# Head norms and memory softmax in place in PSUM, small copies and scalings on ScalarE: a two-layer decoder trunk

## Chip, core and metric

The kernel runs as one program on one core of a Trainium2 chip. The core has TensorE (PE, matmuls into PSUM), VectorE (DVE), ScalarE (ACT), GpSimd (POOL), SyncE (SP, which issues the DMAs), an SBUF and a PSUM of eight banks of 512 fp32 words a partition. The metric is the device time of one execution in microseconds; less is better.

## What is computed

Two decoder layers over 512 tokens of width 1024, and 256 memory tokens. Layer 0 has a gated MLP, a differential attention (8 heads, two score maps each) and a memory cross-attention; layer 1 a convolution branch, a sparse attention and a memory cross-attention. Cut to what the change touches:

```python
def rms_norm(x, g):
    y = xf * lax.rsqrt(jnp.mean(xf * xf, axis=-1, keepdims=True) + EPS)
    return (y * g).astype(x.dtype)

# differential attention: p = softmax(q k^T), two maps of a head
pd = p[:, :, 0] - lam * p[:, :, 1]
o  = einsum('bhqk,bhkd->bhqd', pd, v)

# memory attention, 4 heads of 64
q, k = rms_norm(q, qnorm), rms_norm(k, knorm)
p = jax.nn.softmax(einsum('bshd,bmhd->bhsm', q, k) * HEAD_DIM ** -0.5)
y = einsum('bhsm,bmhd->bshd', p, v)
```

Queries and keys of the differential and of the sparse attention get a partial rotary embedding behind their norm.

## The kernel before

Weights come as 512 KB units by DMA and are split into a high and a low fp32r half (L376 on ACT, L377 on POOL for weights, on DVE for activations read from PSUM). A product is three matmuls (`mm3`, L396 to L398). Projections with tokens on the partitions (`proj_N`) leave each 128-token tile in a PSUM bank of kind "d"; those with features on the partitions (`proj_T`) fill a whole bank.

`head_norm` takes such a PSUM tile `p`: ACT squares it to SBUF (L492), DVE sums (L494), POOL makes the factor `r` by two tiny operations (`rstd`, L370 and L372), and DVE multiplies by the gain or by the rotary table, reading PSUM and writing an SBUF tile `t` (L498, L501), with the rotary parts added in SBUF (L503 to L505). `to_keys` (L511) and `to_queries` (L521) multiply `t` by `r`, SBUF to SBUF, and PE transposes the result (L393). `b_qk` does the same for the differential attention (L873 to L883).

`b_attn` runs 8 heads; in each, the four 128-query tiles in the order 3, 2, 1, 0: scores on PE (L923), mask and row minimum on DVE (L925), exponentials on ACT (L954), reciprocal (L955), the factor `cf` from the two row sums and `nlam`, minus lambda (L957), the difference of the two maps (L958), transposes (L393), a copy (L934) and the output matmuls (L961) into one bank of kind "o" per head.

`m_attn` takes two heads at a time: scores into a bank of kind "s" (L597, L598), row maximum on DVE (L600), two exponentials on ACT from PSUM to an SBUF tile `e` (L603), reciprocal (L604), and two scalings of `e` by `times`: the first on DVE (L572), the second on POOL (L570). Then transposes, a split and the products with the values (L582 to L584). `gate_heads` (L578) multiplies the output by its gate.

`c_taps` is the depthwise convolution of layer 1: four feature tiles of 31 taps. Three of them run on DVE (L1252, then 30 times L1260, accumulating in one PSUM bank of kind "c"), the second on ACT and POOL (L1257, L1258). Each tile begins when its two products are there (L1238 reads the second); the next DVE tile waits for the "c" bank. The taps have a low priority.

The program is written as generators that `merge` interleaves: `b_attn` with the projections of layer 0; `m_attn` of layer 0 with an output projection; in layer 1 `m_attn` with the convolution's projections (`glu`), then `d_kv`, `d_cmp` and `d_q`, then the sparse attention `d_attn`. The order on each engine is not written out by hand: the framework places the instructions by priority on a timeline of its own while it builds, so other instructions or other dependencies can give another order. Engines run their own queues in order and wait on semaphores; the framework orders accesses of two engines to one PSUM bank, where one of them writes, by such waits.

## Time and profile before

| | us |
|---|---|
| three runs | 743.29, 743.4, 739.89; median 743.29 |
| the profiled execution | 742.06 |
| its span in the trace | 740.3 |
| PE busy | 679.5 (92%) |
| DVE busy | 530.4 (72%) |
| ACT busy | 366.7 (50%) |
| POOL busy | 390.5 (53%) |

The profile is of one execution. Its span runs from the first to the last instruction; 1.76 us of its time lie around the span. PE is in use nearly throughout, but unevenly: the table by stage among the rows below shows where it waits. Times in the rows are us from the start of the span unless they are marked as a mean in ns.

### The profile page before, as it was taken

To read this page: it belongs to the slowest core of one execution; us is meant where nothing else is said; L and a number is where in the kernel's file an instruction comes from. 1 tells how busy PE (TensorE), PEld (TensorE's weight loads), DVE (VectorE), ACT (ScalarE), POOL (GpSimd) and SP (SyncE) were. 2 spreads that over 40 slices of the span, in tenths; PEclk is the share of its full clock that TensorE was granted. 3 is DMA by queue.
4 is the path that set the end of the run, shared out by engine and by line. 5 is a ranking of instruction groups with operands and counts; after the bars stand their busy time and mean duration, and the time that the engine had idled before them with its cause. 6 is when DMAs were issued, how large, how long until landed. Compare 5 with 4: busy or idle time off the path is not lost.

```text
span 740.3 us, 10929 instructions
## 1 busy us (share of the span) xinstructions
PE 679.5 (92%) x3819; PEld 574.2 (78%) x3819; DVE 530.4 (72%) x1216; ACT 366.7 (50%) x819; POOL 390.5 (53%) x343
## 2 busy tenths in 40 slices
PE   5999999999999898999899898896679989999997
PEld 3889998788898777888787687674457878778876
DVE  5507798777777697853669939999436776889774
ACT  5345345565565564633444465523413646575541
POOL 3376985645347487425565599856143423421440
PEclk9999999999999999999999999999688999999999
DMA  8442244542231434212223112041021100120111
GB/s 315 151 150 78 60 149 119 173 137 91 72 115 58 170 123 163 86 58 62 86 96 105 57 32 84 1 145 55 0 85 58 58 29 30 58 84 3 58 71 72
DMA packets 22375, 66.55 MB, mean 90 GB/s; under 512 B 3504, under 2 KB 3760, under 8 KB 22320
## 3 DMA queue, kind: packets, MB, share of 16 engines
q1 hardware_dynamic: 22320, 65.86, 26.9%
q8 instruction: 30, 0.49, 0.3%
q14 instruction: 25, 0.20, 0.1%
HBM read 57.46 MB, written 2.10 MB: 80 GB/s over the span
## 4 chain that ended last, share of the span: by engine, by line
PE 61%; DVE 25%; POOL 5%; ACT 4%; issue 3%; DMA 1%; SPq 0%; ACTq 0%; DVEq 0%; POOLq 0%
PE banks L397 16%; PE banks L396 15%; PE banks L398 15%; PE banks L393 5%; DVE banks L1260 4%; DVE arena_r L377 3%; PE banks L923 3%; ACT arena_r L376 2%; PE banks L1211 2%; POOL arena_r L377 2%; POOL arena_f L372 2%; DMA arena_f<-in_wall_dram 1%; DVE arena_f L925 1%; DVE arena_f L572 1%; POOL arena_f L1258 1%
## 5 line engine op out<-in xcount | busy, mean ns | idle before, releaser
L396 PE MATMUL banks<-arena_r 128*128 128x512 f32 (+2 forms) x784 | 293.7, 381 | 14.4 <-DVE arena_f L473 4.8
L397 PE MATMUL banks<-arena_r 128*128 128x512 f32 (+2 forms) x784 | 293.8, 377 | 4.9 <-POOL arena_r L377 4.8
L377 POOL TENSOR_TENSOR arena_r<-arena_f,arena_r 128x1024 fp32r<-128x1024 f32 (+2 forms) x87 | 211.7, 2442 | 161.5 <-ACT arena_r L376 160.9
L398 PE MATMUL banks<-arena_r 128*128 128x512 f32 (+2 forms) x784 | 292.3, 376 | 1.1 <-POOL arena_r L377 1.1
L396 PEld LDWEIGHTS banks<-arena_r 128*128 128x128 f32 x784 | 151.3, 194 | 40.2 <-DVE arena_f L473 6.2
L397 PEld LDWEIGHTS banks<-arena_r 128*128 128x128 f32 x784 | 151.9, 194 | 30.1 <-POOL arena_r L377 6.4
L398 PEld LDWEIGHTS banks<-arena_r 128*128 128x128 f32 x784 | 151.6, 194 | 25.4 <-POOL arena_r L377 2.0
L376 ACT ACTIVATE arena_r<-arena_f 128x1024 fp32r<-128x1024 f32 (+2 forms) x131 | 110.3, 854 | 94.4 <-PE banks L398 27.7
L393 PE MATMUL banks<-const,arena_f 128*128 128x128 f32 x507 | 84.8, 284 | 29.4 <-DVE arena_f L521 9.4
L393 PEld LDWEIGHTS banks<-const,arena_f 128*128 128x128 f32 x507 | 62.7, 147 | 41.1 <-DVE arena_f L521 9.9
L376 ACT ACTIVATE arena_r<-banks 128x512 fp32r<-128x512 f32 (+1 forms) x112 | 58.2, 532 | 55.9 <-PE banks L393 41.6
L377 DVE TENSOR_TENSOR arena_r<-banks,arena_r 128x512 fp32r<-128x512 f32 (+1 forms) x112 | 67.1, 606 | 21.0 <-ACT arena_r L376 20.6
L925 DVE CUSTOM_DVE_ANT_0 arena_f<-banks,const 128x512 f32<-128x512 f32 (+3 forms) x128 | 60.5, 483 | 29.1 <-PE banks L923 17.0
L570 POOL TENSOR_SCALAR arena_f<-arena_f 128x256 f32<-128x256 f32 (+3 forms) x48 | 29.8, 627 | 90.9 <-DVE arena_f L1190 49.2
L372 POOL TENSOR_TENSOR arena_f<-arena_f,const 128x4 f32<-128x4 f32 (+3 forms) x60 | 68.5, 1143 | 3.7
L1260 DVE SCALAR_TENSOR_TENSOR banks<-arena_f,const,banks 128x482 f32<-128x482 f32 (+14 forms) x90 | 66.0, 733 | 1.6
L954 ACT ACTIVATE arena_f<-arena_f 128x512 f32<-128x512 f32 (+3 forms) x64 | 35.8, 560 | 43.0 <-DVE arena_f L925 42.8
L923 PE MATMUL banks<-arena_r 128*128 128x256 f32 (+7 forms) x192 | 51.1, 338 | 1.8 <-DVE arena_f L925 1.6
L653 DVE TENSOR_TENSOR arena_f<-arena_f,banks 128x512 f32<-128x512 f32 x40 | 27.3, 683 | 30.1 <-PE banks L398 29.9
L1188 ACT ACTIVATE arena_f<-arena_f 128x256 f32<-128x256 f32 (+3 forms) x64 | 35.6, 558 | 23.2 <-DVE arena_f L925 22.7
L370 POOL TENSOR_SCALAR arena_f<-arena_f 128x4 f32<-128x4 f32 (+3 forms) x60 | 19.2, 320 | 41.1 <-ACT arena_f L406 12.9
L1258 POOL TENSOR_TENSOR arena_f<-arena_f 128x482 f32<-128x482 f32 (+29 forms) x30 | 38.2, 1273 | 1.8
(175 smaller groups left out, 836.7 us busy)
## 6 DMA issues: line engine op xcount, KB each, us to landing
arena_f<-in_wall_dram SPq DMA_DIRECT2D x88, 512.0 KB, 3.3
arena_r<-arena_r SPq DMA_DIRECT2D x96, 64.0 KB, 2.0
arena_f<-in_x_dram SPq DMA_DIRECT2D x7, 512.0 KB, 4.6
arena_f<-in_w_dram SPq DMA_DIRECT2D x4, 512.0 KB, 3.9
out_dram<-arena_f SPq DMA_DIRECT2D x8, 256.0 KB, 2.0
arena_f<-in_norms_dram SPq DMA_DIRECT2D x3, 512.0 KB, 4.7
arena_f<-in_mem_dram SPq DMA_DIRECT2D x2, 512.0 KB, 3.2
arena_f<-in_wqb_dram SPq DMA_DIRECT2D x2, 420.0 KB, 3.1
```

The lines of the kernel that those rows point to most:

```text
L372: G.tensor_tensor(r, v, mhalf[:parts, :n], ALU.pow)
L376: act(h, src, AF.Copy)
L377: (eng or V).tensor_tensor(l, src, f32(h), SUB)
L393: nc.tensor.transpose(o, i, ident[:k, :k])
L396: mm(o, lh, rh, start=first, stop=False)
L397: mm(o, lh, rl, start=False, stop=False)
L398: mm(o, ll, rh, start=False, stop=last)
L923: mm(t[:, a % per, :], q, k[:, :w], start=b == 0, stop=b == len(qk) - 1)
L925: V.tensor_tensor_reduce(e[a], t[:, a % per, :], cmask[:, S - w:], -1.0, -NEG, ADD, ALU.min, nm[:, a:a + 1])
L954: act(e[m], e[m], AF.Exp, bias=nm[:, m:m + 1], scale=-1.0, accum_out=l[:, i, m:m + 1])
L1258: G.tensor_tensor(acc[:, z:], acc[:, z:], t[:, z:], ADD)
L1260: V.scalar_tensor_tensor(acc[:, z:], hc[:, :S - z], cw[:, f, k:k + 1], acc[:, z:], MUL, ADD)
```

## The change

Four things, with the line numbers of the kernel before:

- In `head_norm` and `b_qk` the multiplication by gain or table, and the rotary additions, write back into the PSUM tile; the small product `u` moves ahead of them. The last multiplication by `r` (L511, L521, L883) reads PSUM. The PSUM bank is in use until then.
- In `m_attn` the exponentials write into the score bank; the first scaling, on DVE, and the second, now on ACT, read it and write the SBUF tile `e`.
- In `b_attn` ACT copies `nlam` once per head into a spare column of the head's output bank, and L957 reads it there.
- In `d_cmp` eight copies go from DVE to ACT, with the factor 0.5 in them, and one ACT instruction goes; in `m_q1` the small scaling of the gates (L1134) goes from DVE to ACT.

ACT has 35 instructions more, DVE 12 fewer, POOL 16 fewer; PE and the DMAs have the same ones.

```diff
@@ head_norm
         act(sq, p3, AF.Square)
+        if rope is not None:
+            cg, sg = rope
+            u = sc([P, nh, 16])
+            V.tensor_tensor(u, p3[:, :, 0:16], bc(sg.unsqueeze(1), [P, nh, 16]), MUL)
         ss = sc([P, nh])
         V.tensor_reduce(ss, sq, AX.X, ADD)
         r = rstd(sc, ss, 1.0 / 64, nh)
-        t = sq
         if rope is None:
-            V.tensor_tensor(t, p3, bc(gain.unsqueeze(1), [P, nh, 64]), MUL)
+            V.tensor_tensor(p3, p3, bc(gain.unsqueeze(1), [P, nh, 64]), MUL)
         else:
...
+            V.tensor_tensor(p3, p3, bc(cg.unsqueeze(1), [P, nh, 64]), MUL)
+            V.tensor_tensor(p3[:, :, 0:8], p3[:, :, 0:8], u[:, :, 8:16], ADD)
+            V.tensor_tensor(p3[:, :, 8:16], p3[:, :, 8:16], u[:, :, 0:8], ADD)
+        return p3, r, sq
@@ to_queries
-        V.tensor_tensor(t, t, bc(r.unsqueeze(2), [P, nh, 64]), MUL)
+        V.tensor_tensor(t, q3, bc(r.unsqueeze(2), [P, nh, 64]), MUL)
@@ m_attn
                     for j in range(2):
-                        act(e[:, j, :], s[:, j, :], AF.Exp, bias=nm[:, j:j + 1], accum_out=l[:, j:j + 1])
+                        act(s[:, j, :], s[:, j, :], AF.Exp, bias=nm[:, j:j + 1], accum_out=l[:, j:j + 1])
                     V.reciprocal(l, l)
-                    for j in range(2):
-                        times(e[:, j, :], l[:, j:j + 1], SCALE_M[j])
+                    V.tensor_scalar(e[:, 0, :], s[:, 0, :], l[:, 0:1], None, MUL)
+                    act(e[:, 1, :], s[:, 1, :], AF.Copy, scale=l[:, 1:2])
@@ b_qk
-                V.tensor_tensor(t, p4, bc(bcg[:, i, :, :].unsqueeze(2), [P, 2, 4, 32]), MUL)
                 u = sc([P, 2, 4, 8])
                 V.tensor_tensor(u, p4[:, :, :, 0:8], bc(bsg[:, i, :, :].unsqueeze(2), [P, 2, 4, 8]), MUL)
...
+                V.tensor_tensor(p4, p4, bc(bcg[:, i, :, :].unsqueeze(2), [P, 2, 4, 32]), MUL)
+                V.tensor_tensor(p4[:, :, :, 0:4], p4[:, :, :, 0:4], u[:, :, :, 4:8], ADD)
+                V.tensor_tensor(p4[:, :, :, 4:8], p4[:, :, :, 4:8], u[:, :, :, 0:4], ADD)
+                V.tensor_tensor(t3, p.rearrange("p (j d) -> p j d", d=32), bc(r.unsqueeze(2), [P, 8, 32]), MUL)
@@ b_attn
-            o = osc.ps("o", [P, NT, 64])
+            ob = osc.ps("o", [P, NT + 1, 64])
+            o, lam = ob[:, 0:NT, :], ob[:, NT, 0:1]
+            act(lam, nlam, AF.Copy)
...
-                    V.scalar_tensor_tensor(cf, l[:, i, 0:1], nlam, rl[:, i, 1:2], MUL, MUL)
+                    V.scalar_tensor_tensor(cf, l[:, i, 0:1], rl[:, i, 1:2], lam, MUL, MUL)
@@ d_cmp
-                vs = sc([64, 64])
-                act(vs, o, AF.Copy, scale=0.5)
...
-                        V.tensor_copy(cbd[32 * r:32 * r + 32, g, r, :], vs[32 * g:32 * g + 32, :])
+                        act(cbd[32 * r:32 * r + 32, g, r, :], o[32 * g:32 * g + 32, :], AF.Copy, scale=0.5)
@@ m_q1
-                V.tensor_scalar(dgt[:, i, :, :].rearrange("p h b -> p (h b)"), th, 0.5, 0.5, MUL, ADD)
+                act(dgt[:, i, :, :].rearrange("p h b -> p (h b)"), th, AF.Copy, scale=0.5, bias=0.5)
```

How the instructions stand now, at three places, the first on PE and DVE, the others on DVE. In the rows `banks` is PSUM and `arena_f` and `arena_r` are SBUF; line numbers are those of the kernel that the rows come from, and behind L1252 the change's are three less.

The first place is the fourth head of `b_attn`, where its tiles 2 and 1 are worked on. L393 is a tile's transposes, L961 its output matmuls, and between the two stands the copy L934 on ACT; each L961 waits for it. On PE, before, with the semaphores that a row waits for (`DVE_49` counts instructions of DVE, `PE_49` of PE, and so on):

```order
L961 MATMUL banks<-arena_f 128x64 [waits Activation_49]
L961 MATMUL banks<-arena_f 128x64 x3
L393 MATMUL banks<-const,arena_f 128x128 [waits DVE_49]
L393 MATMUL banks<-const,arena_f 128x128
L396 MATMUL banks<-arena_r 128x512
L397 MATMUL banks<-arena_r 128x512
L398 MATMUL banks<-arena_r 128x512
L396 MATMUL banks<-arena_r 128x512
L397 MATMUL banks<-arena_r 128x512
L398 MATMUL banks<-arena_r 128x512
L961 MATMUL banks<-arena_f 128x64 [waits Activation_49]
L961 MATMUL banks<-arena_f 128x64 x2
```

And now, on PE too (L921 is the score matmul that was L923):

```order
L398 MATMUL banks<-arena_r 128x512
L961 MATMUL banks<-arena_f 128x64 [waits Activation_49]
L961 MATMUL banks<-arena_f 128x64 x2
L921 MATMUL banks<-arena_r 128x384 [waits DVE_49]
L393 MATMUL banks<-const,arena_f 128x128 [waits DVE_49]
L393 MATMUL banks<-const,arena_f 128x128
L961 MATMUL banks<-arena_f 128x64 [waits Activation_49]
L961 MATMUL banks<-arena_f 128x64
L396 MATMUL banks<-arena_r 128x512 [waits DVE_49]
```

Before, the rows are tile 3's L961, tile 1's transposes (two), six products, and tile 2's L961; tile 1's own L961 came eight instructions behind. Now tile 2's L961 comes first, one score matmul stands between it and tile 1's transposes, and nothing between these and tile 1's L961. DVE at the same place, before:

```order
L925 ISA arena_f<-banks,const 128x256 [waits PE_49]
L925 ISA arena_f 128x1
L976 TENSOR_TENSOR arena_f<-banks,arena_f 128x4x64 [waits Pool_49]
L925 ISA arena_f<-banks,const 128x128 [waits PE_49]
L925 ISA arena_f 128x1
L955 RECIPROCAL arena_f<-arena_f 128x2 [waits Activation_49]
L957 SCALAR_TENSOR_TENSOR arena_f<-arena_f,const 128x1 [waits DVE_49]
L958 SCALAR_TENSOR_TENSOR arena_f<-arena_f 128x256 [waits DVE_49]
```

And now (L923 is the mask and row minimum that was L925):

```order
L957 SCALAR_TENSOR_TENSOR arena_f<-arena_f,banks 128x1 [waits PE_49]
L958 SCALAR_TENSOR_TENSOR arena_f<-arena_f 128x384 [waits DVE_49]
L957 SCALAR_TENSOR_TENSOR arena_f<-arena_f,banks 128x1 [waits PE_49]
L923 ISA arena_f<-banks,const 128x512 [waits Activation_49]
L923 ISA arena_f 128x1
L958 SCALAR_TENSOR_TENSOR arena_f<-arena_f 128x256 [waits DVE_49]
L955 RECIPROCAL arena_f<-arena_f 128x2 [waits Activation_49]
L473 SCALAR_TENSOR_TENSOR arena_f<-arena_f,banks 128x512 [waits Activation_49]
L957 SCALAR_TENSOR_TENSOR arena_f<-arena_f,banks 128x1 [waits PE_49]
```

L957 waited for DVE's own reciprocal; in 24 of its 32 instances it now waits for PE, and the instruction that it waits for is the last L961 of the head's tile before, which writes the bank that holds lambda. Over all eight heads: between a tile's last transpose and its first L961 stood at least 7 other matmuls in 24 of the 26 places where L961 waits for its copy, and 2 and 3 in the other two; now there are 31 such places, and the numbers are 0 in ten of them, 1 to 3 in six, 5 in one, and 7 or more in fourteen. Between the last L961 of a tile and the transposes that wait for it by way of L957 and L958 stand now (22 places, of which there were none) 0 to 4 matmuls in twelve, and 7 or more in ten; the twelve have 19 in all between them, and the sixteen with 0 to 3 have 12.

The second place is the end of the memory attention of layer 1, where the third convolution tile starts (L1238, then L1252 and L1260; in the changed kernel L1235, L1249 and L1257). L600 (now L598) is the row maximum of a pair of heads. Before:

```order
L600 TENSOR_REDUCE arena_f<-banks 128x2 x2
L1260 SCALAR_TENSOR_TENSOR banks<-arena_f,const,banks 128x511
L604 RECIPROCAL arena_f<-arena_f 128x2
L572 TENSOR_SCALAR arena_f<-arena_f 128x256
L578 SCALAR_TENSOR_TENSOR arena_f<-banks,arena_f 64x2x128 x2
L604 RECIPROCAL arena_f<-arena_f 128x2
L572 TENSOR_SCALAR arena_f<-arena_f 128x256
L377 TENSOR_TENSOR arena_r<-banks,arena_r 128x512 x2
L1238 SCALAR_TENSOR_TENSOR arena_f<-arena_f,banks 128x512
L1252 TENSOR_SCALAR banks<-arena_f,const 128x512
```

And now:

```order
L602 RECIPROCAL arena_f<-arena_f 128x2
L603 TENSOR_SCALAR arena_f<-banks,arena_f 128x256
L1235 SCALAR_TENSOR_TENSOR arena_f<-arena_f,banks 128x512
L1249 TENSOR_SCALAR banks<-arena_f,const 128x512
L1257 SCALAR_TENSOR_TENSOR banks<-arena_f,const,banks 128x482
L598 TENSOR_REDUCE arena_f<-banks 128x2
L377 TENSOR_TENSOR arena_r<-banks,arena_r 128x512
L1257 SCALAR_TENSOR_TENSOR banks<-arena_f,const,banks 128x483
```

The third tile's taps started behind the whole memory attention and now start ahead of its last pair of heads; on PE the product that L1235 reads ends 59 instructions earlier in the queue (instruction 2318 instead of 2377).

The third place is the end of `d_q`, with the last taps of the fourth convolution tile. Before:

```order
L521 TENSOR_TENSOR arena_f<-arena_f 128x512
L504 TENSOR_TENSOR arena_f<-arena_f 128x8x8
L505 TENSOR_TENSOR arena_f<-arena_f 128x8x8
L530 TENSOR_TENSOR arena_r<-banks,arena_r 64x2x128 x2
L1260 SCALAR_TENSOR_TENSOR banks<-arena_f,const,banks 128x511
L521 TENSOR_TENSOR arena_f<-arena_f 128x512
```

And now, from the last tap on:

```order
L1257 SCALAR_TENSOR_TENSOR banks<-arena_f,const,banks 128x511
L503 TENSOR_TENSOR banks<-banks,const 128x512
L496 TENSOR_TENSOR arena_f<-banks,const 128x128
L498 TENSOR_REDUCE arena_f<-arena_f 128x8
L504 TENSOR_TENSOR banks<-banks,arena_f 128x8x8
L503 TENSOR_TENSOR banks<-banks,const 128x512
L505 TENSOR_TENSOR banks<-banks,arena_f 128x8x8
L504 TENSOR_TENSOR banks<-banks,arena_f 128x8x8
L521 TENSOR_TENSOR arena_f<-banks,arena_f 128x512
```

The last tap stood just ahead of the last of the four query tiles' L521; it now stands ahead of the first tile's. From the sparse attention on every engine has the order that it had.

## Rows read from the trace of the kernel before

**Rows 1.** Table by stage: stretch, its length, busy time (instructions) by engine, PE's clock.

```profile
core 0: us, PE busy (x) PEld busy (x) DVE busy (x) ACT busy (x) POOL busy (x), PEclk, DMA share, GB/s
60.00:288.00 228.00, 218.41 (x1353) 193.48 (x1352) 175.80 (x442) 123.16 (x294) 148.12 (x134) 0.98 0.38 119
288.00:376.00 88.00, 85.82 (x517) 73.40 (x516) 49.73 (x92) 39.44 (x87) 39.16 (x36) 1.00 0.20 66
376.00:424.00 48.00, 43.57 (x251) 36.47 (x249) 46.84 (x74) 22.12 (x56) 27.59 (x21) 1.00 0.30 99
424.00:448.00 24.00, 24.00 (x129) 19.88 (x129) 11.53 (x22) 16.26 (x28) 23.06 (x18) 1.00 0.16 47
448.00:510.00 62.00, 56.85 (x300) 46.15 (x299) 59.63 (x106) 27.18 (x46) 47.23 (x40) 0.97 0.23 76
510.00:528.00 18.00, 4.59 (x22) 2.82 (x19) 16.39 (x43) 9.02 (x24) 8.12 (x9) 0.65 0.00 0
```

**Rows 2.** PE, ACT and DVE, 157 to 162, timeline: start, duration, engine, line.

```profile
160.28 0.49 PE L393 MATMUL banks<-const,arena_f 128*128 128x128 f32 x3
...
160.85 0.74 ACT L934 ACTIVATE arena_f<-banks 128x256 f32<-128x256 f32 x2
...
161.65 1.33 PE L961 MATMUL banks<-arena_f 128*128 128x64 f32 x10 [0.47 <-ACT arena_f L934]
```

**Rows 3.** L957 and L934 in layer 0: count, ns min/median/max; then forms.

```profile
L957 DVE SCALAR_TENSOR_TENSOR arena_f<-arena_f,const x32: 202/219/2055, 105.0 to 267.1; 128x1 f32<-128x1 f32 x32
L934 ACT ACTIVATE arena_f<-banks x32: 255/432/600, 108.6 to 278.6; 128x512 f32<-128x512 f32 x8, 128x384 f32<-128x384 f32 x8, 128x256 f32<-128x256 f32 x8, 128x128 f32<-128x128 f32 x8
```

**Rows 4.** Groups of DVE, 60 to 288: busy us, mean ns | idle before.

```profile
L957 DVE SCALAR_TENSOR_TENSOR arena_f<-arena_f,const 128x1 f32<-128x1 f32 x32 | 17.5, 550 | 0.7
L883 DVE TENSOR_TENSOR arena_f<-arena_f 128x256 f32<-128x256 f32 x16 | 14.0, 874 | 6.4 <-POOL arena_f L372 6.4
L958 DVE SCALAR_TENSOR_TENSOR arena_f<-arena_f 128x512 f32<-128x512 f32 x8 | 7.0, 873 | 0.2
L958 DVE SCALAR_TENSOR_TENSOR arena_f<-arena_f 128x128 f32<-128x128 f32 x8 | 6.9, 865 | 0.1
L958 DVE SCALAR_TENSOR_TENSOR arena_f<-arena_f 128x384 f32<-128x384 f32 x8 | 4.9, 614 | 0.2
L958 DVE SCALAR_TENSOR_TENSOR arena_f<-arena_f 128x256 f32<-128x256 f32 x8 | 3.9, 483 | 0.2
```

**Rows 5.** Timeline of PE: instructions that it waited for, idle time and releaser in brackets.

```profile
97.50 0.41 PE L393 MATMUL banks<-const,arena_f 128*128 128x128 f32 x2 [1.12 <-DVE arena_f L883]
280.31 0.79 PE L396 MATMUL banks<-arena_r 128*128 128x512 f32 x1 [2.46 <-DVE arena_f L498]
514.38 0.66 PE L393 MATMUL banks<-const,arena_f 128*128 128x128 f32 x4 [3.92 <-DVE arena_f L521]
520.50 1.41 PE L393 MATMUL banks<-const,arena_f 128*128 128x128 f32 x5 [5.46 <-DVE arena_f L521]
```

**Rows 6.** Timeline of DVE and POOL, 392 to 400.

```profile
392.32 2.40 POOL L377 TENSOR_TENSOR arena_r<-arena_f,arena_r 128x1024 fp32r<-128x1024 f32 x1
393.02 1.99 DVE L521 TENSOR_TENSOR arena_f<-arena_f 128x256 f32<-128x256 f32 x1
396.76 0.41 DVE L521 TENSOR_TENSOR arena_f<-arena_f 128x256 f32<-128x256 f32 x1
```

**Rows 7.** Groups of DVE, 374 to 522: busy us, mean ns | idle before.

```profile
L572 DVE TENSOR_SCALAR arena_f<-arena_f 128x256 f32<-128x256 f32 x8 | 7.3, 908 | 0.1
L521 DVE TENSOR_TENSOR arena_f<-arena_f 128x256 f32<-128x256 f32 x2 | 2.4, 1200 | 0.0
L1134 DVE TENSOR_SCALAR const<-arena_f 128x24 f32<-128x24 f32 x2 | 2.1, 1030 | 0.0
L498 DVE TENSOR_TENSOR arena_f<-banks,const 128x256 f32<-128x256 f32 x2 | 0.7, 412 | 0.0
```

**Rows 8.** The last query tile's factor on POOL and its multiplication on DVE.

```profile
513.52 1.64 POOL L372 TENSOR_TENSOR arena_f<-arena_f,const 128x8 f32<-128x8 f32 x1
519.75 0.69 DVE L521 TENSOR_TENSOR arena_f<-arena_f 128x512 f32<-128x512 f32 x1
```

More of the change, by code (lines that the diff above doesn't have):

```diff
@@ L495, in head_norm, with to_keys @@
         r = rstd(sc, ss, 1.0 / 64, nh)
-        t = sq
         if rope is None:
-            V.tensor_tensor(t, p3, bc(gain.unsqueeze(1), [P, nh, 64]), MUL)
+            V.tensor_tensor(p3, p3, bc(gain.unsqueeze(1), [P, nh, 64]), MUL)
         else:
-            cg, sg = rope
-            V.tensor_tensor(t, p3, bc(cg.unsqueeze(1), [P, nh, 64]), MUL)
-            u = sc([P, nh, 16])
-            V.tensor_tensor(u, p3[:, :, 0:16], bc(sg.unsqueeze(1), [P, nh, 16]), MUL)
-            V.tensor_tensor(t[:, :, 0:8], t[:, :, 0:8], u[:, :, 8:16], ADD)
-            V.tensor_tensor(t[:, :, 8:16], t[:, :, 8:16], u[:, :, 0:8], ADD)
-        return t, r
-    def to_keys(sc, t, r, h, l):
+            V.tensor_tensor(p3, p3, bc(cg.unsqueeze(1), [P, nh, 64]), MUL)
+            V.tensor_tensor(p3[:, :, 0:8], p3[:, :, 0:8], u[:, :, 8:16], ADD)
+            V.tensor_tensor(p3[:, :, 8:16], p3[:, :, 8:16], u[:, :, 0:8], ADD)
+        return p3, r, sq
+    def to_keys(sc, t, r, _, h, l):
         d = sc([P, 4, 2, 64])
@@ L516, in to_keys, with to_queries @@
         split(p, h, l)
-    def to_queries(sc, t, r, dst):
+    def to_queries(sc, q3, r, t, dst):
         nh = t.shape[1]
-        V.tensor_tensor(t, t, bc(r.unsqueeze(2), [P, nh, 64]), MUL)
+        V.tensor_tensor(t, q3, bc(r.unsqueeze(2), [P, nh, 64]), MUL)
         p = sc.ps("t", [P, nh // 2, P])
@@ L557, in mem_kv @@
             with SC() as sc:
-                t, r = head_norm(sc, p[:, 0:256], 4, mkg[layer], None)
-                to_keys(sc, t, r, kt[:, 0, :, tok(i)], kt[:, 1, :, tok(i)])
+                to_keys(sc, *head_norm(sc, p[:, 0:256], 4, mkg[layer], None), kt[:, 0, :, tok(i)], kt[:, 1, :, tok(i)])
             yield UT
@@ L564, in m_query @@
         with SC() as sc:
-            t, r = head_norm(sc, p, 4, mqg[layer], None)
-            to_queries(sc, t, r, [qs[:, :, tok(i)]])
+            to_queries(sc, *head_norm(sc, p, 4, mqg[layer], None), [qs[:, :, tok(i)]])
     def times(e, f, eng):
@@ L1039, in d_kv @@
             with SC() as sc:
-                t, r = head_norm(sc, p[:, 0:256], 4, None, (dcg[:, i, 1, :], dsg[:, i, 1, :]))
-                to_keys(sc, t, r, dkh[:, :, tok(i)], dkl[:, :, tok(i)])
+                to_keys(sc, *head_norm(sc, p[:, 0:256], 4, None, (dcg[:, i, 1, :], dsg[:, i, 1, :])), dkh[:, :, tok(i)], dkl[:, :, tok(i)])
             yield UT + 440
@@ L1046, in d_q @@
             with SC() as sc:
-                t, r = head_norm(sc, p, 8, None, (dcg[:, i, 0, :], dsg[:, i, 0, :]))
+                n = head_norm(sc, p, 8, None, (dcg[:, i, 0, :], dsg[:, i, 0, :]))
                 qsc = SC()
@@ L1050, in d_q @@
                 dqs[i] = (q, qsc)
-                to_queries(sc, t, r, [q[:, 0:4, :], q[:, 4:8, :]])
+                to_queries(sc, *n, [q[:, 0:4, :], q[:, 4:8, :]])
             yield UT + 880
@@ L1365 @@
 PTILE, WIDE = 1, 2
-SCALE_D, SCALE_M = "vp", "vp"
+SCALE_D = "vp"
 CD, CX = 80, 3600
```

3 lines of the change are left out of this document (removed).

## Prediction

> **What bounds the kernel now.** I read the page's table of busy time first, then the table by stage [rows 1], then the timeline of PE for its waits, and last the groups of DVE in the two stages where PE waits for it. In the table by stage PE is busy 218.41 of 228 us from 60 to 288, 85.82 of 88 in the next stage and 43.57 of 48 from 376 to 424, all at a granted clock near 1.00: the time is made by PE's own queue, and a wait that is put into this queue costs its length. From 424 to 510 the taps keep DVE at work (11.53 of 24, where it waits for PE, then 59.63 of 62) and PE waits a little; from 510 to 528 PE is busy 4.59 of 18 and waits for DVE, twice named: 3.92 and 5.46 us for L521 [rows 5]. So an edit counts in layer 0 if it touches what PE waits for between tiles, and in layer 1 if it shortens DVE.
>
> **The change part by part.** *Lambda in the bank of "o".* Before, L957 waited for nothing on PE, and DVE ran several tiles ahead of the output matmuls. Now 24 of 32 wait for the last L961 of the tile before, so a head is a chain: L961, L957, L958, transposes, copy L934, L961. The order shows what that does to PE's queue. In sixteen places at most three matmuls stand between a tile's transposes and its L961 (before: two places), in twelve at most four between the last L961 and the transposes that wait for it by way of DVE (before: none). PE can't pass these links, since its queue runs in order.
>
> The price of a link is read from its parts. Copy: the transposes end at 160.28 + 0.49 = 160.77, the copy starts 0.08 later at 160.85, and its pair ends at 161.59, 0.06 ahead of L961, which had PE idle for 0.47 us [rows 2]. One copy has a median of 0.43 [rows 3], so a link is 0.08 + 0.43 + 0.06 = 0.57. Sixteen make 9.1 us; the 12 matmuls that stand in them cover, at 218.41 us / 1353 = 0.16 us each [rows 1], 1.9 us. That leaves 7.2.
> DVE: L957 takes 0.22 when undisturbed [rows 3], L958 (7.0 + 6.9 + 4.9 + 3.9) / 32 = 0.71 [rows 4], with the same two handovers of 0.07: 1.07. Twelve make 12.8; the 19 matmuls between cover 3.0. That leaves 9.8. Copy and DVE links together: 17.0, less the 0.47 that PE paid before.
> The mean of L957 is 0.55 [rows 4], 0.33 above its median [rows 3]; the rest is waiting that L958, which stands behind it and reads two SBUF tiles too, will take over. So reading lambda from PSUM gains nothing, and I don't count the 10.6 us (32 x 0.33) as a gain.
> Behind a waiting L957 stand on DVE the row minima, the additions of the projections' products and the splits that PE's next products read. At the fourth head L957 of tile 1 directly follows L958 of tile 2, and DVE waits there for transposes, copy and L961, some 1.7 us by rows 2. No row of before has this wait. Its cost to PE lies between 0 (DVE is idle 52 us of the 228 [rows 1]) and half a us at each of the 24, 12 us. I take the middle, 6, since DVE was three quarters busy and PE's queue has no slack. Sum of the lambda edit: 17.0 - 0.5 + 6 = +22.5.
>
> *b_qk and head_norm in place.* L883 takes 874 ns and read two SBUF tiles; reading PSUM it should take about 412, as L498 does at that size from PSUM [rows 7], 16 x 0.46 = 7.4 us less on DVE. Of this PE sees what it waited for: 1.12 us at 97.50. The other wait in layer 0, 2.46 us for a bank that L498 released [rows 5], I let go too, as the order there is another. Gain 3.6; bounds 0 (the banks are now held until the last multiplication) and 3.6.
>
> *Memory attention and small copies.* The tie to POOL is seen at 392.32: while its split runs for 2.40 us, an L521 that takes 0.41 alone takes 1.99 [rows 6]. In 374 to 522 L572 at 908 instead of 412 ns is 8 x 0.50 = 4.0 us, L521 2 x 0.79 = 1.6, and L1134, which goes to ACT, 2.1 [rows 7]: 7.7 us off DVE. ACT has room (22.12 of 48 [rows 1]). In 376 to 424 PE waits 48 - 43.57 = 4.4 us in all; I let 3.0 of it go, about two thirds, as it is not all for DVE (bounds 0 and 4.4).
> The memory attention of layer 0 lies where PE is full: 0, both ways. The copies of `d_cmp` go to ACT, idle there: 0. Should ACT be late, its copy is as short as L934's, some 0.4 us each.
>
> *Taps and the tail.* The order now has the last tap ahead of the first query tile's L521. The last factor is ready on POOL at 513.52 + 1.64 = 515.16, and its L521 starts at 519.75 [rows 8], 4.6 us late because of what stands ahead of it on DVE. I let these 4.6 go (bounds 0 and 4.6); what is late next is POOL's factor. Behind 528 the order is that of before: 0.
>
> [...]
>
> **The sum** is made against the profiled execution, 742.06, which is 1.23 below the median of 743.29: 742.06 + 22.5 - 3.6 - 3.0 - 4.6 = **753.4**, of which 751.6 is the span.
>
> **The rivals.**
> - *The links fall into time that PE idles anyway.* PE's idle time in 60 to 288 is 9.6 us [rows 1], and DVE has 7.4 us less work there. If the links take all of this and DVE is never late, the lambda edit costs 17.0 - 9.6 = 7.4, and with the gains of 3.6, 4.4 and 4.6 the time is 742.06 - 5.2 = 736.9, faster than before. It decides from the point where layer 0 loses less than the 7.6 to 9.0 us that layer 1 gains. For it: most of that idle time has no large wait to its name. Against: a link is a chain from PE to PE, so it has to add its length wherever PE has nothing else in its queue.
> - *The links cost their own length and DVE isn't late behind L957.* Then the 6 us go: 747.4; with L958 at 0.41, as an L521 that POOL leaves alone [rows 6], instead of 0.71 (12 x 0.3 = 3.6 less), 743.8, no change.
> - *DVE late everywhere.* The 12 us instead of 6, the banks of `b_qk` held longer (no gain of 3.6), and DVE's lead for layer 1 without effect on PE (0 of 7.6): 742.06 + 17.0 - 0.5 + 12 = 770.6. For it: 24 waits of 1.7 us are 41 us, four fifths of DVE's idle time. Against: part of the 24 finds PE already through.
> - *The change doesn't do what it says in layer 1.* DVE is freed, but PE is held there by DMA, ACT or POOL: then the 3.0 and the 4.6 stay and the time is 761.
>
> **How the numbers follow.** 0.5% of the median is 3.7 us, about what a measurement of this kernel can tell from no change: faster is below 739.6, slower above 747.0. Forecast and neighbours from 747 to 765, with layer 1 idle or not: 0.64. DVE late everywhere, above 765: 0.08. No change, 739.6 to 747: 0.14. Links absorbed, below 739.6: 0.14. Hence slower 0.72, same 0.14, faster 0.14. The range leaves out most of the two outer cases: 740 to 768; its ends are the absorbed links with only half of the gains, and the late DVE.
>
> **What would show it.** In the changed kernel's table by stage the stretch from 60 to 288 must be longer, by 15 to 20 us at PE's unchanged busy time, and PE's idle time there must be named: ACT L934's successor before L961 and DVE L958 before transposes, some 0.5 to 1 us each, a dozen and more of each. L957 must have PE as its releaser, with DVE idle ahead of it. L883 and L572 must fall to about 0.4 us in the groups, and PE's two waits of 3.92 and 5.46 must shrink together by 4 to 5. It is wrong if PE's busy share in layer 0 stays at 96%: then the links are covered, and the time comes out below 747. It is wrong in size if products (L396) wait for DVE's splits or for banks more often than the links do.

## The result and the profile after

The changed kernel takes 801.01 us (median of 4 runs, 800.29 to 802.76) against 743.31: a ratio of 1.0789, 95% interval 1.0767 to 1.0810. The direction was forecast, the size was not: +58 us instead of +11. The profiled execution has a span of 798.6 us.

The table by stage of the changed kernel, cut at the same events as [rows 1] or near them (first score matmul of layer 0's memory attention, first product of the taps, last tap, first scores of the sparse attention); columns as there:

```profile
core 0: us, PE busy (x) PEld busy (x) DVE busy (x) ACT busy (x) POOL busy (x), PEclk, DMA share, GB/s
60.00:363.10 303.10, 258.00 (x1370) 215.50 (x1369) 170.52 (x446) 128.01 (x303) 145.14 (x136) 0.87 0.29 91
363.10:451.90 88.80, 85.67 (x508) 73.17 (x507) 48.21 (x88) 43.31 (x98) 35.16 (x25) 0.98 0.19 61
451.90:567.30 115.40, 114.79 (x648) 96.76 (x647) 106.36 (x192) 65.82 (x132) 88.69 (x67) 1.00 0.26 88
567.30:620.10 52.80, 38.00 (x152) 29.07 (x151) 24.50 (x61) 17.11 (x44) 19.29 (x19) 0.77 0.16 50
620.10:798.60 178.50, 167.09 (x933) 139.24 (x932) 135.31 (x370) 97.12 (x237) 59.47 (x50) 0.98 0.15 51
```

and of the kernel before, the last three stages at these cuts:

```profile
376.40:519.70 143.30, 125.14 (x679) 102.83 (x677) 127.49 (x222) 69.18 (x137) 102.11 (x81) 0.97 0.23 74
519.70:561.80 42.10, 31.65 (x119) 23.70 (x120) 17.73 (x40) 9.20 (x22) 12.20 (x12) 0.73 0.16 50
561.80:740.30 178.50, 167.17 (x933) 139.22 (x931) 135.35 (x370) 96.85 (x237) 60.56 (x50) 0.98 0.15 51
```

Layer 0's first part grew from 228.0 to 303.1 us, 75.1 more. Its number of matmuls is about the same (1353 and 1370). PE's idle time in it rose from 9.6 to 45.1, 35.5 us, and its busy time from 218.4 to 258.0, 39.6 us, while the granted clock fell from 0.98 to 0.87. The stretches in which the clock is at its lower level (0.50) are nine in the changed kernel and three in the kernel before, with these sums (length in us, then the busy time of each engine):

```profile
sum 78.52, PE 61.93 PEld 46.91 DVE 43.37 ACT 24.96 POOL 25.52; mean PE 6.88 PEld 5.21 DVE 4.82 ACT 2.77 POOL 2.84
```

```profile
sum 10.24, PE 9.93 PEld 7.99 DVE 5.97 ACT 5.60 POOL 4.39; mean PE 3.31 PEld 2.66 DVE 1.99 ACT 1.87 POOL 1.46
```

PE is busy at half the clock for 52.0 us more. Half of that, 26 us, a third of the 75.1, is an estimate of what the lower clock costs: products start every 0.43 us at 213 to 215 us in the same trace, where the clock is 0.50, and every 0.23 at 216 to 218, where it is 1.00. The other 13.6 us of busy time I put down to 17 matmuls more ahead of the cut and to matmuls that stand alone behind a wait: at 121 us in the same trace products of 0.39 us follow each other every 0.23, and one that stands alone counts whole.

The dense stage (from the first score matmul to the first product of the taps) stayed (88.4, 88.8). The two stages of the taps and of `d_cmp` together fell from 185.4 to 168.2, 17.2 us gained, and behind them nothing moved (178.5 both). 75.1 + 0.4 - 17.2 = 58.3, the difference of the two spans.

PE's waits in the changed kernel, 60 to 363 (line, releaser, us in all, times, longest):

```profile
PE banks L393 <- DVE arena_f L958: 16.8, 9, 5.5
PE banks L921 <- DVE arena_f L923: 11.8, 15, 2.2
PE banks L961 <- ACT arena_f L932: 5.8, 12, 0.7
PE banks L396 <- DVE arena_f L511: 2.7, 2, 2.5
```

The links of the prediction are the first and the third row (L932 is the copy that was L934). The second has 0.9 us in the kernel before: PE waits for the row minima (L923, before L925), some of which stand on DVE behind a waiting L957. What DVE does there, by groups (busy us, mean ns | idle before):

```profile
L958 DVE SCALAR_TENSOR_TENSOR arena_f<-arena_f 128x256 f32<-128x256 f32 x8 | 12.1, 1515 | 0.1
...
L957 DVE SCALAR_TENSOR_TENSOR arena_f<-arena_f,banks 128x1 f32<-128x1 f32 x32 | 6.8, 213 | 37.8 <-PE banks L961 35.9 <-ACT banks L948 1.6
L881 DVE TENSOR_TENSOR arena_f<-banks,arena_f 128x256 f32<-128x256 f32 x16 | 6.7, 420 | 4.5 <-POOL arena_f L372 4.3
```

L957 itself is never slow now (213 ns; 550 in [rows 4]), but DVE stands idle 35.9 us ahead of it for PE. L958, 483 ns at 256 elements in [rows 4], now takes 1515: it took over the waiting for POOL. Of its 32 instances 14 take longer than is usual at their size (0.78 to 2.58 us, where the other 18 take 0.33 to 0.75), and all 14 run beside an instruction of POOL, as here, with the transposes behind it:

```profile
122.59 2.34 POOL L377 TENSOR_TENSOR arena_r<-arena_f,arena_r 128x1024 fp32r<-128x1024 f32 x1 [3.94 <-ACT arena_r L376]
...
122.64 2.57 DVE L958 SCALAR_TENSOR_TENSOR arena_f<-arena_f 128x256 f32<-128x256 f32 x1
...
125.27 0.44 PE L393 MATMUL banks<-const,arena_f 128*128 128x128 f32 x2 [2.53 <-DVE arena_f L958]
```

L881, which was L883, takes 420 instead of 874.

One turn of the chain, third head, as the timeline shows it:

```profile
177.52 0.22 DVE L957 SCALAR_TENSOR_TENSOR arena_f<-arena_f,banks 128x1 f32<-128x1 f32 x1 [1.16 <-PE banks L961]
...
177.77 1.06 DVE L958 SCALAR_TENSOR_TENSOR arena_f<-arena_f 128x384 f32<-128x384 f32 x1
...
178.48 2.08 PE L850 MATMUL banks<-arena_f 128*128 128x128 f32 x8 [0.99 <-POOL arena_f L834]
...
180.35 0.85 PE L393 MATMUL banks<-const,arena_f 128*128 128x128 f32 x3
...
181.24 0.49 ACT L932 ACTIVATE arena_f<-banks 128x384 f32<-128x384 f32 x1 [5.07 <-PE banks L393]
...
181.78 1.54 PE L961 MATMUL banks<-arena_f 128*128 128x64 f32 x6 [0.58 <-ACT arena_f L932]
...
183.36 0.22 DVE L957 SCALAR_TENSOR_TENSOR arena_f<-arena_f,banks 128x1 f32<-128x1 f32 x1 [0.42 <-PE banks L961]
```

Each step starts within 0.1 us of the end of the one before, on another engine, but for the transposes: they start 1.5 us after L958, behind eight matmuls of the gated MLP (L850), which had waited 0.99 us for POOL. 181.24 to 181.78 is the copy link, 0.58 us of waiting for PE (0.57 in the prediction). L961 takes 1.54 us for six matmuls here, at a clock of 0.50; at 121.55 in the same trace, at 1.00, six take 0.78.

The longest of PE's waits, 5.49 us, is no link of this chain. It lies at the change from the third head to the fourth (L976 is the last reading of the third head's outputs, L948 the copy of lambda for the fourth):

```profile
206.68 0.42 DVE L976 TENSOR_TENSOR arena_f<-banks,arena_f 128x256 f32<-128x256 f32 x1 [4.18 <-POOL arena_f L975]
207.13 0.17 ACT L948 ACTIVATE banks<-const 128x1 f32<-128x1 f32 x1 [3.87 <-DVE arena_f L976]
207.34 0.22 DVE L957 SCALAR_TENSOR_TENSOR arena_f<-arena_f,banks 128x1 f32<-128x1 f32 x1 [0.24 <-ACT banks L948]
...
208.40 1.12 PE L393 MATMUL banks<-const,arena_f 128*128 128x128 f32 x4 [5.49 <-DVE arena_f L958]
```

The granted clock around this place, in stretches of 8 us (columns as above):

```profile
164.00:172.00 8.00, 3.96 (x12) 2.21 (x11) 4.20 (x15) 4.84 (x15) 4.14 (x6) 0.74 0.40 113
172.00:180.00 8.00, 6.20 (x24) 5.02 (x25) 4.15 (x9) 1.47 (x4) 0.64 (x1) 0.50 0.57 173
180.00:188.00 8.00, 6.64 (x22) 5.05 (x22) 3.36 (x11) 3.84 (x10) 0.00 (x0) 0.50 0.02 7
188.00:196.00 8.00, 8.00 (x39) 6.48 (x38) 3.14 (x9) 3.43 (x7) 2.92 (x2) 0.98 0.00 1
```

PE is idle for 4.04 us of the first stretch; the clock is then at its lower level (0.50) for 16 us, in which PE does 24 and 22 matmuls, and back near the higher one (0.98) with 39 matmuls in the fourth. Of the nine stretches at the lower level this one is the longest, some 20 us.

### The profile page after: what moved, and what is told of

It is laid out like the page before. It is cut to its first block, busy times and chain, and to the rows that moved or that the text cites. A ratio compares the mean times of both kernels' runs of the same rounds, so it can differ in the third digit from the quotient of the medians.

```text
span 798.6 us, 10919 instructions
## 1 busy us (share of the span) xinstructions
PE 713.4 (89%) x3819; PEld 594.2 (74%) x3819; DVE 508.3 (64%) x1204; ACT 379.4 (48%) x854; POOL 375.7 (47%) x327
## 4 chain that ended last, share of the span: by engine, by line
PE 69%; DVE 16%; ACT 6%; POOL 3%; issue 3%; DMA 2%; SPq 0%; ACTq 0%; DVEq 0%; POOLq 0%
PE banks L396 18%; PE banks L397 18%; PE banks L398 18%; PE banks L393 5%; DVE arena_r L377 3%; PE banks L921 3%; ACT arena_r L376 2%; PE banks L961 2%; DMA arena_f<-in_wall_dram 2%; PE banks L1208 2%; POOL arena_r L377 2%; DVE arena_f L958 1%; DVE arena_f L923 1%; DVE banks L1257 1%; POOL arena_f L372 1%
## 5 line engine op out<-in xcount | busy, mean ns | idle before, releaser
L396 PE MATMUL banks<-arena_r 128*128 128x512 f32 (+2 forms) x784 | 299.6, 387 | 13.2 <-DVE arena_f L473 4.1
L397 PE MATMUL banks<-arena_r 128*128 128x512 f32 (+2 forms) x784 | 300.1, 383 | 3.5 <-POOL arena_r L377 3.3
L398 PE MATMUL banks<-arena_r 128*128 128x512 f32 (+2 forms) x784 | 297.3, 381 | 0.2 <-DVE arena_r L377 0.2
L396 PEld LDWEIGHTS banks<-arena_r 128*128 128x128 f32 x784 | 154.3, 198 | 42.7 <-DVE arena_f L473 6.3
L397 PEld LDWEIGHTS banks<-arena_r 128*128 128x128 f32 x784 | 155.6, 198 | 29.1 <-POOL arena_r L377 4.3
L398 PEld LDWEIGHTS banks<-arena_r 128*128 128x128 f32 x784 | 155.0, 198 | 25.9 <-DVE arena_r L377 0.7
L376 ACT ACTIVATE arena_r<-arena_f 128x1024 fp32r<-128x1024 f32 (+2 forms) x131 | 110.6, 855 | 129.9 <-PE banks L397 33.2
L393 PE MATMUL banks<-const,arena_f 128*128 128x128 f32 x507 | 87.5, 294 | 40.5 <-DVE arena_f L958 16.8
L393 PEld LDWEIGHTS banks<-const,arena_f 128*128 128x128 f32 x507 | 63.6, 150 | 53.7 <-DVE arena_f L958 19.9
L923 DVE CUSTOM_DVE_ANT_0 arena_f<-banks,const 128x512 f32<-128x512 f32 (+3 forms) x128 | 61.2, 486 | 44.5 <-PE banks L921 19.8
L377 DVE TENSOR_TENSOR arena_r<-banks,arena_r 128x512 fp32r<-128x512 f32 (+1 forms) x112 | 67.2, 608 | 21.0 <-ACT arena_r L376 20.6
L921 PE MATMUL banks<-arena_r 128*128 128x256 f32 (+7 forms) x192 | 55.9, 358 | 14.7 <-DVE arena_f L923 12.6
L1257 DVE SCALAR_TENSOR_TENSOR banks<-arena_f,const,banks 128x482 f32<-128x482 f32 (+14 forms) x90 | 66.2, 735 | 1.6
L568 POOL TENSOR_SCALAR arena_f<-arena_f 128x512 f32<-128x512 f32 (+3 forms) x32 | 20.0, 631 | 70.3 <-DVE arena_f L1187 46.0
L921 PEld LDWEIGHTS banks<-arena_r 128*128 128x128 f32 (+1 forms) x192 | 34.3, 196 | 23.8 <-DVE arena_f L923 18.5
L370 POOL TENSOR_SCALAR arena_f<-arena_f 128x4 f32<-128x4 f32 (+3 forms) x60 | 15.4, 257 | 54.3 <-DVE arena_f L498 19.8
```

Source lines behind the costliest of these rows:

```text
L376: act(h, src, AF.Copy)
L377: (eng or V).tensor_tensor(l, src, f32(h), SUB)
L393: nc.tensor.transpose(o, i, ident[:k, :k])
L396: mm(o, lh, rh, start=first, stop=False)
L397: mm(o, lh, rl, start=False, stop=False)
L398: mm(o, ll, rh, start=False, stop=last)
```

## The experiments

Each kernel was timed against the kernel before on its chip (741.6 to 742.5 us there); the time is a median, the interval that of the ratio. "Layer 0" below is the stretch from 60 us to the first score matmul of the memory attention, "dense stage" the one from there to the first product of the taps.

**Lambda undone.** The changed kernel with

```diff
-            act(lam, nlam, AF.Copy)
-                    V.scalar_tensor_tensor(cf, l[:, i, 0:1], rl[:, i, 1:2], lam, MUL, MUL)
+                    V.scalar_tensor_tensor(cf, l[:, i, 0:1], nlam, rl[:, i, 1:2], MUL, MUL)
```

> The changed kernel with lambda read from SBUF again (no copy on ScalarE, no spare column), all else as changed. Theory: the 24 waits of L957 for TensorE make all of the loss in layer 0, 75 us between 60 us and the first score matmul of the memory attention (35.5 us more idle, 39.6 us more busy at a lower granted clock), and the rest of the change gains the 17 us that the two traces differ by from the first tap to the sparse attention. Then 722 to 728 us, clock of the core 0.98 or more. Rival: the norms in place hold the PSUM banks of the projections and starve TensorE in layer 0; then 760 us or more, with the memory attention of layer 0 starting after 320 us.

Measured 732.04 us, ratio 0.9876 (0.9862 to 0.9891), clock 0.967; layer 0 225.2 us, 11.0 of them idle. Lambda alone makes the loss, 69.0 us here, and without it the kernel takes 1.2% less than before. It missed the expected 722 to 728: layer 0 and the dense stage together take 323.4 us where the kernel before takes 316.4, and the changed kernel, in which lambda covers this, had not shown it. The two can't be compared one by one, since 1332 matmuls stand ahead of the cut here and 1370 in the changed kernel.

**Lambda alone.** The kernel before with the opposite edit.

> The kernel before with the lambda edit alone. Theory: +75 us in layer 0 and nothing gained later: 810 to 820 us, granted clock 0.92. Rival (norms in place are to blame): 740 to 750 us. A third way, the loss needs both edits (banks held by the norms and a DVE that waits): between 755 and 790 us.

817.41 us, ratio 1.1028 (1.1009 to 1.1047); layer 0 303.3 us, 42.8 idle, clock 0.87. As expected: +75.8 without any norm in place.

**Lambda in half of the heads.** `lam if n >= 4 else nlam` in L957.

> The changed kernel with lambda read from PSUM in the last four heads only (12 waits of L957 for TensorE instead of 24; the copies stay in all heads). Theory, each wait costs its own: half of the 75 us, 760 to 768 us. Rival, the clock falls only when waits are dense over a long stretch: the loss is not proportional, under 750 us.

765.85 us, ratio 1.0321 (1.0296 to 1.0347): 33.8 above undo_lam, 49% of its 69.0. The loss grows with the number of heads that read it.

**Lambda for the first tile only.** `lam if a == 0 else nlam`.

> The changed kernel with the copy of lambda into the bank of the outputs kept in all heads, but read there only for the first tile of each head, where no matmul has written the bank yet; the other three tiles read SBUF. It tells the copy and the spare column from the waits. Theory (waits): as undo_lam within 3 us, 722 to 730. Rival (the copy itself or its bank on ScalarE's queue): 790 to 801 us.

756.52 us, ratio 1.0201 (1.0171 to 1.0231). Neither: 24.5 us above undo_lam, though no L957 waits for a matmul. So my theory lacked a piece. Its timeline shows it, at the change from one head to the next (L968 squares the head's output, L970 sums, L975 is its factor on POOL, L976 the last reading of the bank, L948 the copy of lambda):

```profile
131.67 0.38 ACT L968 ACTIVATE arena_f<-banks 128x256 f32<-128x256 f32 x1
...
132.08 0.42 DVE L970 TENSOR_REDUCE arena_f<-arena_f 128x4 f32<-128x256 f32 x1
...
135.78 0.42 DVE L976 TENSOR_TENSOR arena_f<-banks,arena_f 128x256 f32<-128x256 f32 x1 [1.09 <-POOL arena_f L975]
...
136.24 0.17 ACT L948 ACTIVATE banks<-const 128x1 f32<-128x1 f32 x1 [0.79 <-DVE arena_f L976]
...
136.45 0.21 DVE L957 SCALAR_TENSOR_TENSOR arena_f<-arena_f,banks 128x1 f32<-128x1 f32 x1 [0.24 <-ACT banks L948]
```

There is one bank of kind "o". The next head's lambda can be copied only when the last head's output has been squared, summed, scaled and read, 4.8 us from L968 to L957, and the next head's first difference waits for the copy. Before, only the first L961 of the next head needed the bank, some steps later. PE idles 18.8 us more in layer 0 than in the kernel before, under several names; the three rows of the changed kernel that I had as links and as a late DVE are here

```profile
PE banks L921 <- DVE arena_f L923: 8.5, 9, 2.0
...
PE banks L961 <- ACT arena_f L932: 3.3, 3, 2.6
...
PE banks L393 <- DVE arena_f L958: 2.0, 1, 2.0
```

so that most of the waiting for the row minima stands here too, without any wait for L961.

**The copy without its reading.** The copy stays, all L957 read `nlam`.

> The changed kernel with ScalarE's copy of lambda into the bank of the outputs in every head, but L957 reading SBUF in all 32 tiles. It tells the copy from the reading. There is one such bank, so the copy waits until DVE has read the head before, and stands in ScalarE's queue. Theory: the copy alone makes most of what lam_first lost (756.5 against 732.0): 750 to 757 us, with ScalarE waiting for DVE L976 ahead of L948. Rival: the reading by the first tile ties the heads together: 732 to 736 us.

731.78 us, ratio 0.9859 (0.9843 to 0.9876), as undo_lam. The theory of the waiting copy fell: ACT does wait for L976 (10.6 us in four places), but nobody needs it. The rival (732 to 736) had it, to 0.2 us: the reading by the first tile costs lam_first's 24.7 us over this, the other 24 readings, added to it, the 44.5 from there to the changed kernel.

**Lambda in a bank of its own**, which the projections lose (`P_L0` (2, 2, 2, 2)), and the same without reading it.

> The changed kernel with lambda in a PSUM bank of its own, copied there once ahead of the eight heads; the projections have two banks instead of three for it. L957 reads PSUM and waits for TensorE nowhere. Theory (the loss is the sharing of a bank with the output matmuls): within 3 us of its control lam_own_ctl, whatever that takes with a bank less; 735 to 755 us. Rival (a read from PSUM is what costs): 20 us or more above the control.

> As lam_own, with the same banks and the same single copy, but L957 reads lambda in SBUF. It is the control: undo_lam (732.0) with one bank less for the projections. Both theories: 733 to 755 us.

763.96 us (759.8 to 766.64) and 766.71 (766.46 to 767.66); ratios 1.0288 (1.0238 to 1.0339) and 1.0336 (1.0319 to 1.0352). Both missed the expected 733 to 755: the missing bank costs more than I had thought (the control is 34.7 us above undo_lam). But the reading from PSUM costs nothing against the control: what costs is that the bank is shared with the output matmuls. L957 (here L958) and the difference behind it (L959) by groups, first with lambda in PSUM, then in the control:

```profile
L959 DVE SCALAR_TENSOR_TENSOR arena_f<-arena_f 128x512 f32<-128x512 f32 (+3 forms) x32 | 25.7, 806 | 0.6
...
L958 DVE SCALAR_TENSOR_TENSOR arena_f<-arena_f,banks 128x1 f32<-128x1 f32 x32 | 6.8, 211 | 0.6
```

```profile
L959 DVE SCALAR_TENSOR_TENSOR arena_f<-arena_f 128x512 f32<-128x512 f32 (+3 forms) x32 | 20.1, 630 | 0.6
...
L958 DVE SCALAR_TENSOR_TENSOR arena_f<-arena_f,const 128x1 f32<-128x1 f32 x32 | 18.7, 584 | 0.6
```

Of the 11.9 us that the small product no longer waits, the difference behind it takes over 5.6. The two times aren't far enough apart for a verdict.

**Gaps filled.** To tell waiting from the clock, the gaps of the changed kernel were filled with matmuls that nobody reads, a number between L958 and the transposes and as many behind these: six of 32 columns (fill6), two and five of 160 columns (fill_wide, fill_wide5).

```diff
+            for k in range(6 if fill is not None else 0):
+                mm(fill, ident, ident[:, 0:32], start=True, stop=True)
```

> The changed kernel with 12 small matmuls more per tile of the differential attention, six between L957 and the tile's transposes and six behind these; they write an unused column range of the outputs' bank and are read by nobody. They add some 384 matmuls of about 0.1 us, 40 us of work, where TensorE stands idle now. Theory: the granted clock falls because TensorE stands idle; with the gaps filled the clock of layer 0 rises from 0.87 to 0.95 or more, and the time is at or below that of the changed kernel, 780 to 801 us, in spite of the added work. Rival: the clock has another cause (the mix of work); it stays at 0.87 to 0.89 and the time rises by what isn't hidden, 810 to 840 us.

> As fill6, but with two matmuls of 160 columns in each gap instead of six of 32 (128 in all). fill6 kept TensorE busy (17 us idle in layer 0 instead of 45) at a granted clock of 0.89. Theory: it is columns that keep the clock, not occupancy: in layer 0 the clock rises to 0.93 or more and the time is 780 to 800 us. Rival: the clock stays at 0.87 to 0.89 and the time is over 801 us.

> As fill_wide, with five matmuls of 160 columns in each gap, 320 in all, so that the gaps are closed as far as fill6 closed them (17 us idle in layer 0). Theory (columns keep the clock, occupancy doesn't): clock of layer 0 at 0.95 or more, against 0.89 in fill6. Rival: 0.92 or less. The time is above 801 us in either case, since the added work, some 60 us, exceeds the gaps; it is the clock that tells.

Layer 0 of the three, in this order:

```profile
60.00:421.10 361.10, 344.07 (x2150) 312.81 (x2149) 167.40 (x445) 130.97 (x303) 142.80 (x132) 0.89 0.24 75
```

```profile
60.00:378.10 318.10, 282.97 (x1637) 248.93 (x1636) 168.50 (x444) 127.47 (x302) 142.61 (x131) 0.92 0.27 85
```

```profile
60.00:399.90 339.90, 319.31 (x2020) 289.83 (x2019) 165.82 (x445) 130.76 (x302) 142.94 (x131) 0.97 0.25 80
```

The times are 858.95, 817.16 and 837.72 us, ratios 1.1576 (1.1544 to 1.1609), 1.1005 (1.0975 to 1.1035) and 1.1304 (1.1271 to 1.1337). fill6 missed its expectation: the idle time fell from 45 to 17 us, yet the clock only rose from 0.87 to 0.89. I had put its work at 40 us where PE's busy time grew by 86: each of the 384 matmuls stands as two in the trace (768 records at their two lines), and each of the two adds 0.11 us. With the five wider ones 20.6 us stayed idle and the clock was 0.97, as expected. So with the narrow matmuls in the gaps the clock of layer 0 stayed at 0.89, and with the wider ones in the same gaps it came to 0.97, against 0.98 before. fill_wide lies between and decides nothing alone; its time missed the expected 780 to 800. In all three the added work is more than what the clock gave back, so no run shows what layer 0 takes with the waits and without the lower clock: the 26 us above stay an estimate.

**The rest of the change by parts.** mattn_copies: the memory softmax and all small copies alone. hn_only: `head_norm` in place alone. hn_rope: in place only where it has a rotary table. hn_rope_mattn: that and mattn_copies. undo_lam_bqk: the changed kernel without lambda and without `b_qk` in place.

```diff
-                V.tensor_tensor(p4, p4, bc(bcg[:, i, :, :].unsqueeze(2), [P, 2, 4, 32]), MUL)
+                V.tensor_tensor(t, p4, bc(bcg[:, i, :, :].unsqueeze(2), [P, 2, 4, 32]), MUL)
...
```

> The kernel before with the memory softmax in place, its second scaling on ScalarE and the small copies on ScalarE; norms and lambda as before. Theory: the 28 us that the stage of the taps loses come from this part (DVE is no longer held by GpSimd at L572, and the taps start earlier), 11 of them are given back in the stage behind, and layer 0 stays: 742 - 17 = 723 to 728 us, faster than undo_lam (732). Rival: the norms in place free DVE in that stage; then 738 to 743 us.

> The changed kernel with lambda from SBUF, and with the norm of the differential attention's queries and keys (b_qk) through SBUF as before; the other norms and all else as changed. From 60 us to the first tap's product undo_lam takes 323 us where before took 316. Theory: b_qk in place costs these 7 us (each bank is held until its last multiplication): 725 us, with the stretch at 316 to 318. Rival: they come from the memory norms in place or from the order of the dense stage: 730 to 734 us.

> The kernel before with head_norm in place, for all its callers, and nothing else of the change. undo_lam_bqk (728.7) has this and the memory softmax and the copies; those two alone made nothing (741.9). Theory: head_norm in place makes the whole gain, because the sparse attention's norms come off DVE's queue earlier and without the waits for GpSimd: 726 to 731 us. Rival: the gain needs both, since only together do the taps end ahead of the norms: 736 to 743 us.

> As hn_only, but in place only where the norm has a rotary table (keys and queries of the sparse attention); the memory norms stay in SBUF. From the first score matmul of layer 0's memory attention to the first tap's product undo_lam, undo_lam_bqk and copy_only take 98 us where before and mattn_copies take 88 to 90. Theory: the memory norms in place cost these 9 us: 10 us less than hn_only, with the stretch at 88 to 90. Rival: the memory norms have no part in it: as hn_only within 2 us.

> As undo_lam_bqk, with the memory norms through SBUF as before: in place are the sparse attention's norms and the memory softmax, the copies are on ScalarE. Theory: 9 to 10 us less than undo_lam_bqk, 719 to 721 us, the fastest of all. Rival: 727 to 731 us.

| kernel | us | ratio, interval | layer 0 | dense stage | taps to sparse scores |
|---|---|---|---|---|---|
| before | 741.6 to 742.5 | | 228.0 | 88.4 | 185.4 |
| mattn_copies | 741.87 | 0.9990 (0.9979 to 1.0002) | 228.2 | 90.3 | 183.3 |
| hn_rope | 738.44 | 0.9947 (0.9929 to 0.9965) | 228.0 | 88.3 | 183.0 |
| hn_only | 737.70 | 0.9934 (0.9911 to 0.9957) | 222.5 | 97.8 | 178.1 |
| hn_rope_mattn | 736.78 | 0.9924 (0.9897 to 0.9950) | 229.3 | 90.3 | 177.8 |
| undo_lam | 732.04 | 0.9876 (0.9862 to 0.9891) | 225.2 | 98.2 | 168.8 |
| undo_lam_bqk | 728.72 | 0.9818 (0.9800 to 0.9836) | 222.5 | 97.7 | 167.7 |

The expectation for mattn_copies (723 to 728) fell, although its first scaling, L572 before, is as fast as in the changed kernel. So did that for hn_only (726 to 731): the gain needs both. The taps of the third convolution tile start 62.8 us after those of the first in the kernel before and in hn_rope, 59.8 in hn_only, 55.3 in mattn_copies and hn_rope_mattn, and 46.9 in undo_lam, undo_lam_bqk and the changed kernel, which have memory norms and memory softmax both in place. 15.9 us earlier is nearly the whole 17.2. Why the two together do more than their sum (3.0 + 7.5) no run tells apart; the order on the engines differs in each, and I leave it open.

With the memory norms in place the dense stage is 9.4 us longer (hn_only against before) and layer 0 5.5 shorter. But the cut lies elsewhere: 1330 matmuls stand ahead of it in hn_only, 1353 before, and 543 and 520 behind it, in the dense stage. In hn_only the two stages are

```profile
60.00:282.50 222.50, 210.97 (x1330) 186.58 (x1328) 173.04 (x437) 121.57 (x292) 140.31 (x130) 0.99 0.36 113
282.50:380.30 97.80, 93.99 (x543) 80.05 (x544) 55.51 (x98) 41.14 (x90) 45.79 (x40) 0.97 0.23 80
```

Together they take 320.3 us against 316.4, and that says what the memory norms cost there: 3.9 us, not the 9 to 10 of my expectations. So hn_rope isn't 10 us below hn_only but equal to it within 2, as its rival had it, and hn_rope_mattn, at 736.78, missed the 719 to 721 as well as its rival's 727 to 731. `b_qk` in place costs 3.3 us (undo_lam against undo_lam_bqk), about half of the 7 that I had given it. undo_lam_bqk, 1.8% below the kernel before, is the fastest here.

## Why the prediction was wrong

**What bounds the kernel.** Right: PE's queue sets layer 0, and the waits that were put into it were paid, 35.5 us more of idle time. The larger of the two steps that failed is this: I read the granted clock near 1.00 in [rows 1] as a constant, and expected the loss "at PE's unchanged busy time". The row for 510 to 528 in the same group, with PE busy 4.59 of 18 us, already had a clock of 0.65. The sum had no term for it. PE's busy time grew by 39.6 of the 75.1 us, an estimated 26 of them by the lower clock, and across the kernels it grows with the waits: 13.3 us more busy time with 18.8 more idle (lam_first against before), 42.1 with 33.2 (lam_only).

**The links.** Sound, and near in size. Copy links: 7.2 forecast, 5.8 measured. DVE links: 9.8 forecast, 16.8 measured. L958 takes over POOL's waiting, its mean over the four sizes is 1.08 us where I had 0.71 from [rows 4], and this lies in the chain; and 5.5 of the 16.8 are no link, but the wait at the change of heads shown above.

**DVE late behind L957.** 6 forecast, with ends of 0 and 12; the row of the waits for L921 shows 11.8 us, the upper end. But lam_first, where no L957 waits for a matmul, has 8.5 us in that row (undo_lam has 1.8). How much of the 11.8 belongs to the 24 waits that I priced, and how much to the change of heads that I didn't, stays open.

**The first tile of each head.** The other step that failed is "24 of 32 wait for the last L961": I took the other eight for free. For six of them DVE stands idle until ACT's copy is there (1.6 us in all), and the copy waits for a bank that the head before still holds; lam_first shows that this reading alone costs 24.7 us, idle and busy time together. The copy's own wait was in the order and I didn't follow it across the head's end.

**Lambda from PSUM gains nothing.** Half right: lam_own shows 5.6 of 11.9 us passing to L958, not all.

**`b_qk` and `head_norm` in place.** The duration came as forecast (420 ns, 412 forecast), the gain of 3.6 us did not. Of its two parts the 1.12 us are gone from the waits, but the 2.46 us for a bank that L498 released [rows 5] are there again, as 2.5 for L511, which now releases it; and with `b_qk` undone the kernel is 3.3 us faster. The lower bound was 0 and excluded that. I had named the held banks, but that they cost the 3.3 us isn't shown: PE idles 11.0 us of layer 0 in undo_lam and 11.4 in undo_lam_bqk, and most of the difference is in its busy time (214.2 and 211.1).

**Layer 1.** 7.6 forecast, 17.2 measured. The 4.6 us of the tail: PE's two waits of 3.92 and 5.46 [rows 5] became one of 6.7, so 2.7 of the 9.4 went there. The 3.0 of 376 to 424 was the mis-sized term: the order showed the third tile's taps 59 instructions earlier on PE, and I told of it as a fact but didn't price it; its start came 15.9 us earlier. The relief of DVE by instruction was right (L572, 908 ns in [rows 7], has become 480 in mattn_copies), but alone it is worth nothing.

**PSUM as a source.** L883 and L572 were forecast at 412 ns, what L498 took from PSUM [rows 7]. L883 came to 420. For L572, now L603, and for L521 these are the groups in the taps' stage of the changed kernel:

```profile
L603 DVE TENSOR_SCALAR arena_f<-banks,arena_f 128x256 f32<-128x256 f32 x8 | 3.9, 481 | 0.1
...
L521 DVE TENSOR_TENSOR arena_f<-banks,arena_f 128x256 f32<-128x256 f32 x2 | 0.8, 421 | 0.0
```

L521 takes 421 ns from PSUM against 0.41 us from SBUF [rows 6]: no difference for this product of two tensors. For the product with a scalar there is one: L603 takes 469 to 485 in its 16 instances, where L572 of before, from SBUF, took 0.34 or 0.35 us in three of its eight instances of that stage, one of them here:

```profile
397.80 0.34 DVE L572 TENSOR_SCALAR arena_f<-arena_f 128x256 f32<-128x256 f32 x1
```

The outer rivals name the right places (DVE late everywhere, 770.6), but without the clock and the change of heads no case reached 801. The ends of the range don't come out of the cases that they are laid to, either: the absorbed links with half of the gains make 743.2, not 740, and the late DVE 770.6, not 768.
